# Hymba layer: weight casts and second-stage operands queued behind named matmuls, rotary shuffles issued from ScalarE

## The chip, the cores and the metric

The kernel runs on one core of a Trainium2 chip. The metric is device time in microseconds. A core has TensorE (PE, with its weight loads PEld), VectorE (DVE), ScalarE (ACT), GpSimd (POOL) and SyncE (SP). Every engine takes its instructions from a queue of its own, in order; engines wait for one another by semaphores. A DMA is an instruction in the queue of the engine that issues it, and the data moves on while the engine goes on.

## What is computed

A decoder layer with two groups of heads. The input `x` (1024 x 2048, float32) is projected by `w_in`; one group does sliding-window softmax attention with rotary positions and a sink, the other gated linear attention (GLA) in chunks; both are gated, concatenated, projected by `w_out`, added to the residual and normalized:

```python
h = jnp.einsum('bsd,de->bse', x, w_in[l])
q_a, k_a, v_a, z_a, q_g, k_g, v_g, z_g, gk_lr = jnp.split(h, pts, axis=-1)
qa = _rope(q_a.reshape(B, S, ATT_HEADS, ATT_HEAD_DIM), cos, sin)
ka = _rope(k_a.reshape(B, S, ATT_KV_HEADS, ATT_HEAD_DIM), cos, sin)
y_a = _swa_sink_attention(qa, ka, va, attn_sinks[l]) * jax.nn.silu(z_a)
...
y = jnp.einsum('bse,ed->bsd', jnp.concatenate([y_a, y_g], axis=-1), w_out[l])
x = _layer_norm(DN_ALPHA * x + y, ln_g[l], ln_b[l])
```

## The kernel before

Every float32 product is made of three matmuls on rounded halves: `split` (line 106) casts a tile to its high half (`wh`, `xh`, on ACT, line 112) and subtracts to get the low half (`wl`, `xl`, on DVE, line 113); then hi·hi, hi·lo and lo·hi are summed in PSUM. Weights are loaded by SP into a `raw` buffer of 128 x 1024 (4 buffers, line 102), which holds two tiles; their halves go to a pool of 8 buffers. Activations' halves have 16 buffers.

Stage 1 runs over two halves of the sequence, 512 positions each. `main_f` (line 171) gives a 128 x 512 tile of transposed projections (`acc`, 48 matmuls), `main_v` (line 183) values in the other orientation (`accv`). Between these projections stand the small works on what they gave: `rope` (line 207) copies a projection to `rq` on ACT, shuffles its four groups of 32 rows by four DMAs from SP into `rs` (line 213), and multiplies by cosine on DVE (line 214) and by sine on POOL (line 215). Attention makes scores `ps`, a mask, a maximum `nm`, exponentials on ACT (line 282), a sum `sm`, a scaling of `s` on POOL (line 285), and transposes `pt` on PE (line 288). The GLA part makes decays `w`: an exponential on ACT (line 353), a product on DVE (line 354), and many small `pa` matmuls on PE (line 372). There are 18 calls of `rope`, so 72 shuffle DMAs.

Stage 2 (from line 880) makes the gates `z` (s = 0) and the output projection (s = 1) by Strassen's seven products each, in steps (s, i), with i in the order 1, 6, 7, 4, 2, 5, 3 and 1, 6, 7, 4, 5, 3, 2. Each step has two column halves `fp` and, in each, eight `k`: `w_part` (line 754) loads and splits a weight tile, `product` (line 766) adds three matmuls to `acco` for each row tile, `collect` moves finished sums out of PSUM. The moving operand of a step is a sum of blocks of `x` or of the mixed heads: `y_part` (line 728) loads two or three blocks `yr` by SP, adds them on POOL (line 749, or 746 for i = 3, where a kept sum is loaded), and splits the result. While the second half `fp == 1` of a step is written down, the operands of the next step are made.

The order in each queue is not that of the code: a scheduler simulates the program with its own costs and places each instruction. `tc.high_priority` (as in `split`) lets it place an instruction as early as its inputs and buffers allow. `order(a, b)` tells it that `a` comes after `b`; across engines this adds no wait on the chip, it only changes where `a` stands in its queue.

Of the kernel before, what the change touches and what calls it, by code (L numbers as in the profile page):

```python
# [21 lines left out]
KT = 16  # L22
# [52 lines left out]
def build(ctx: ExitStack, tc, xT, xr, w_e, w_v, w_z, w_gk, w_up, b_gk, cos_d, sin_d, cst_d, sinks, wn_d, w_out, g_d, b_d, out):  # L75
# [30 lines left out]

    def split(src, pool, tag):
        n = src.shape[-1]
        hi = pool.tile([P, 512], F32R, name=tag + "h", tag=tag + "h")[:, :n]
        lo = pool.tile([P, 512], F32R, name=tag + "l", tag=tag + "l")[:, :n]  # L110
        with tc.high_priority():
            A.copy(hi, src)  # L112
            V.tensor_tensor(lo, src, hi.bitcast(F32), ALU.subtract)  # L113
        return hi, lo

# [54 lines left out]
    def main_f(ws, xs):  # L170
        accs = [mm.tile([P, T], F32, name="acc", tag="mm") for _ in ws]
        for k in range(KT):
            xh, xl = xs[k]
            c = slice((k % 4) * P, (k % 4) * P + P)
            for acc, w in zip(accs, ws):
                wh, wl = w[k // 4]
                first = PE.matmul(acc, wh[:, c], xh, start=(k == 0), stop=False)  # L177
                job_head[0] = first if k == 0 else job_head[0]
                PE.matmul(acc, wh[:, c], xl, start=False, stop=False)  # L179
                PE.matmul(acc, wl[:, c], xh, start=False, stop=(k == KT - 1))  # L180
        return accs

    def main_v(w, xs):
        acc = [mm.tile([P, 2, 256], F32, name="accv", tag="mm") for _ in range(2)]
        for k in range(KT):
            wh, wl = w[k // 2]
            c = slice((k % 2) * 256, (k % 2) * 256 + 256)
            xh, xl = xs[k]
            for tb in range(NB):
                o = acc[tb // 2][:, tb % 2]  # L190
                t = slice(tb * P, tb * P + P)
                first = PE.matmul(o, xh[:, t], wh[:, c], start=(k == 0 and tb % 2 == 0), stop=False, skip_group_check=True)  # L192
                job_head[0] = first if k == 0 else job_head[0]
                PE.matmul(o, xh[:, t], wl[:, c], start=False, stop=False, skip_group_check=True)  # L194
                PE.matmul(o, xl[:, t], wh[:, c], start=False, stop=(k == KT - 1), skip_group_check=True)  # L195
        return acc
# [9 lines left out]
    def rope(acc, tabs):  # L206
# [4 lines left out]
        for a in range(4):  # L211
            b = a ^ 1
            SP.dma_start(sw[32 * a:32 * a + 32], q[32 * b:32 * b + 32])
        V.tensor_tensor(q, q, cos, ALU.mult)
# [512 lines left out]

    def y_part(s, i, k):

# [15 lines left out]
        if i == 3:  # L745
            G.tensor_tensor(a, a, raw(kept, "xl"), ALU.add)
        for n, (h, g) in enumerate(more):
            b = raw(block(h, g), "xl" if n % 2 == 0 else "xh")
            G.tensor_tensor(a, a, b, ALU.subtract)  # L749
        if i == 6:  # L750
            A.dma_start(kept, a)
        return split(a, x_p, "x")

# [12 lines left out]
    def product(acc, s, y, w, t, k, first, last):  # L766

        (lh, ll), (rh, rl) = (y, w) if s else (w, y)
        c = slice(t * P, t * P + P)
        PE.matmul(acc, lh[:, c], rh, start=(first and k == 0), stop=False, skip_group_check=True)  # L770
        PE.matmul(acc, lh[:, c], rl, start=False, stop=False, skip_group_check=True)  # L771
        PE.matmul(acc, ll[:, c], rh, start=False, stop=(last and k == 7), skip_group_check=True)  # L772

# [115 lines left out]
    for n, (s, i) in enumerate(seq[:-1]):  # L889
# [11 lines left out]
        for fp in range(2):  # L901
            if i in FIRST:
                accs[fp] = banks(nb)
            for k in range(8):
                if k % 2 == 0:
                    ws = w_part(s, i, fp, k // 2, w_p, "w")
                    for k2 in (k, k + 1):
                        if fp == 1:
                            ys[(*seq[n + 1], k2)] = y_part(*seq[n + 1], k2)
                        elif (s, i, k2) not in ys:  # L910
                            ys[s, i, k2] = y_part(s, i, k2)
# [73 lines left out]
```

## Times and profile before

| | us |
|---|---|
| runs of the kernel before, median of 3 (lowest, highest) | 1478.41 (1468.97, 1479.26) |
| the profiled execution, its own time | 1467.29 |
| its span | 1465.5 |
| TensorE busy | 1398.5 |
| VectorE busy | 888.9 |
| ScalarE busy | 644.1 |
| GpSimd busy | 278.6 |

The span is the stretch that the trace covers; what lies around it is launch and end. Busy time of TensorE contains its slow stretches too: the granted clock over the span is 0.985 of full speed, and where a table of stretches shows less than 1.00, matmuls ran at half the clock for part of it. Stage 1's projections run to 877 us; stage 2 begins there, while the last attention and GLA works are still under way, and its steps end at 1452 us.

### The profile page before, as it was taken

Reading aid. Unit: us, or ns where it says so; the run is one execution under the profiler, and the core shown is the slowest. Engines: PE = TensorE matmul, PEld = TensorE weight load, DVE = VectorE, ACT = ScalarE, POOL = GpSimd, SP = SyncE. Lnnn points to the kernel's source line nnn. Section 1 sums busy time; section 2 is a strip of 40 time slices with the busy share of each in tenths; the row PEclk is TensorE's granted clock in tenths of the full one; section 3 lists DMA queues with packets and bytes.
Section 4 is the critical chain, followed back from the end, with each engine's and each line's share of the span. In section 5 each row is a group of like instructions: output and inputs, shape, how many; then the busy total and the mean of one; then the engine's idle time right before and its main releaser. Section 6 shows DMA issues by size and latency. Waiting matters only on the chain.

```text
span 1465.5 us, 23449 instructions
## 1 busy us (share of the span) xinstructions
PE 1398.5 (95%) x8848; PEld 1163.7 (79%) x8848; DVE 888.9 (61%) x1559; ACT 644.1 (44%) x1405; POOL 278.6 (19%) x269
## 2 busy tenths in 40 slices
PE   8999999999899999999989996999997999999996
PEld 5888879788676888879778775788885888788885
DVE  5555575665666566575665676336475835465798
ACT  5544544544454544544544554246333424433330
POOL 0011131121121111122121224220112032122000
PEclk9999999999999999999999998999999999999998
DMA  8346463645739848464864656777779887766452
GB/s 311 116 141 183 134 182 94 204 137 151 190 111 303 211 158 229 136 185 121 248 156 132 154 145 196 269 202 224 239 263 309 302 256 242 232 216 194 152 214 115
DMA packets 102818, 284.24 MB, mean 194 GB/s; under 512 B 11825, under 2 KB 26161, under 8 KB 101041
## 3 DMA queue, kind: packets, MB, share of 16 engines
q1 hardware_dynamic: 92720, 249.19, 51.1%
q0 software_dynamic: 7680, 29.36, 11.3%
q10 hardware_dynamic: 2304, 4.20, 0.7%
q8 instruction: 69, 1.13, 0.3%
q14 instruction: 45, 0.36, 0.1%
HBM read 250.72 MB, written 85.98 MB: 230 GB/s over the span
## 4 chain that ended last, share of the span: by engine, by line
PE 73%; DMA 12%; DVE 6%; ACT 2%; issue 2%; SPq 2%; POOL 2%; DVEq 0%; POOLq 0%; ACTq 0%
PE acco L770 9%; PE acco L771 9%; PE acco L772 9%; PE acc L177 8%; PE acc L180 8%; PE acc L179 8%; PE accv L195 4%; PE accv L192 4%; PE accv L194 4%; DMA yr<-yd 3%; DMA rs<-rq 2%; PE po L298 2%; DMA yr<-in_xT_dram 2%; DVE wl L113 2%; DMA yr<-ysum 1%
## 5 line engine op out<-in xcount | busy, mean ns | idle before, releaser
L113 DVE TENSOR_TENSOR wl<-raw,wh 128x512 fp32r<-128x512 f32 (+1 forms) x456 | 316.1, 706 | 170.8 <-ACT wh L112 156.4
L112 ACT CAST wh<-raw 128x512 fp32r<-128x512 f32 (+1 forms) x456 | 262.3, 592 | 221.4 <-PE acc L179 111.7
L177 PE MATMUL acc<-xh,wh 128*128 128x512 f32 x704 | 279.4, 398 | 6.9 <-ACT wh L112 6.9
L180 PE MATMUL acc<-xh,wl 128*128 128x512 f32 x704 | 279.2, 397 | 0.0
L179 PE MATMUL acc<-xl,wh 128*128 128x512 f32 x704 | 279.0, 396 | 0.0
L113 DVE TENSOR_TENSOR xl<-yr,xh 128x512 fp32r<-128x512 f32 x112 | 77.3, 691 | 199.2 <-ACT xh L112 198.7
L112 ACT CAST xh<-yr 128x512 fp32r<-128x512 f32 x112 | 69.4, 620 | 276.3 <-POOL yr L749 171.4
L177 PEld LDWEIGHTS acc<-xh,wh 128*128 128x128 f32 x704 | 134.0, 190 | 36.7 <-ACT wh L112 7.9
L770 PE MATMUL acco<-wh,xh 128*128 128x512 f32 x416 | 161.6, 390 | 0.8 <-ACT xh L112 0.8
L771 PE MATMUL acco<-wl,xh 128*128 128x512 f32 x416 | 161.9, 389 | 0.0
L772 PE MATMUL acco<-wh,xl 128*128 128x512 f32 x416 | 161.6, 389 | 0.0
L180 PEld LDWEIGHTS acc<-xh,wl 128*128 128x128 f32 x704 | 133.6, 190 | 30.4 <-issue 2.1
L179 PEld LDWEIGHTS acc<-xl,wh 128*128 128x128 f32 x704 | 134.0, 190 | 28.6 <-issue 1.4
L195 PE MATMUL accv<-wh,xl 128*128 128x256 f32 x512 | 145.2, 284 | 0.0
L192 PE MATMUL accv<-wh,xh 128*128 128x256 f32 x512 | 145.0, 283 | 0.0
L194 PE MATMUL accv<-wl,xh 128*128 128x256 f32 x512 | 144.9, 283 | 0.0
L770 PE MATMUL acco<-xh,wh 128*128 128x512 f32 x336 | 132.6, 397 | 12.1 <-ACT xh L112 6.6
L749 POOL TENSOR_TENSOR yr<-yr 128x512 f32<-128x512 f32 x64 | 86.4, 1350 | 297.0 <-DMA yr<-yd 131.1
L772 PE MATMUL acco<-xh,wl 128*128 128x512 f32 x336 | 132.6, 396 | 0.7 <-DVE wl L113 0.7
L771 PE MATMUL acco<-xl,wh 128*128 128x512 f32 x336 | 132.7, 395 | 0.2 <-DVE xl L113 0.2
L195 PEld LDWEIGHTS accv<-wh,xl 128*128 128x128 f32 x512 | 97.8, 191 | 0.9 <-issue 0.9
L192 PEld LDWEIGHTS accv<-wh,xh 128*128 128x128 f32 x512 | 97.9, 191 | 0.9 <-issue 0.6
(187 smaller groups left out, 2154.6 us busy)
## 6 DMA issues: line engine op xcount, KB each, us to landing
raw<-in_w_e_dram SPq DMA_DIRECT2D x86, 512.0 KB, 4.6
yr<-in_xT_dram SPq DMA_DIRECT2D x88, 256.0 KB, 4.7
yr<-yd SPq DMA_DIRECT2D x88, 256.0 KB, 5.5
raw<-in_w_v_dram SPq DMA_DIRECT2D x32, 512.0 KB, 5.3
raw<-td SPq DMA_DIRECT2D x32, 512.0 KB, 4.8
td<-in_w_z_dram SPq DMA_DIRECT2D x16, 768.0 KB, 6.8
raw<-td SPq DMA_DIRECT2D x32, 384.0 KB, 3.9
raw<-in_w_out_dram SPq DMA_DIRECT2D x24, 512.0 KB, 4.8
```

Source lines behind the costliest of these rows:

```text
L112: A.copy(hi, src)
L113: V.tensor_tensor(lo, src, hi.bitcast(F32), ALU.subtract)
L177: first = PE.matmul(acc, wh[:, c], xh, start=(k == 0), stop=False)
L179: PE.matmul(acc, wh[:, c], xl, start=False, stop=False)
L180: PE.matmul(acc, wl[:, c], xh, start=False, stop=(k == KT - 1))
L192: first = PE.matmul(o, xh[:, t], wh[:, c], start=(k == 0 and tb % 2 == 0), stop=False, skip_group_check=True)
L194: PE.matmul(o, xh[:, t], wl[:, c], start=False, stop=False, skip_group_check=True)
L195: PE.matmul(o, xl[:, t], wh[:, c], start=False, stop=(k == KT - 1), skip_group_check=True)
L749: G.tensor_tensor(a, a, b, ALU.subtract)
L770: PE.matmul(acc, lh[:, c], rh, start=(first and k == 0), stop=False, skip_group_check=True)
L771: PE.matmul(acc, lh[:, c], rl, start=False, stop=False, skip_group_check=True)
L772: PE.matmul(acc, ll[:, c], rh, start=False, stop=(last and k == 7), skip_group_check=True)
```

## The change

Three things are changed. First, `split` with the tag "w" numbers the weight tiles, `used` records the last matmul so far on each, and the ACT cast of tile n is ordered behind the last matmul on tile n-7. Second, the four shuffle DMAs of `rope` are issued from ACT's queue, not from SP's. Third, `product` keeps the latest matmul in `recent`, and a `y_part` made for the next step orders its POOL sums and its ACT cast behind that matmul. The addition for i = 3 moves into the loop of the sums. Instructions are the same in number and kind, but for the 72 issues that move from SP to ACT. All three orders are of the scheduler's kind described above.

```diff
-    def split(src, pool, tag):
+    ends, made = {}, [0]
+
+    def used(n, ins):
+        if n is not None:
+            ends[n] = ins
+
+    def split(src, pool, tag, behind=None):
...
+        if tag == "w":
+            behind = ends.get(made[0] - 7)
+            made[0] += 1
         with tc.high_priority():
-            A.copy(hi, src)
+            ins = A.copy(hi, src)
+            if behind is not None:
+                order(ins, behind)
             V.tensor_tensor(lo, src, hi.bitcast(F32), ALU.subtract)
-        return hi, lo
+        return (hi, lo, made[0] - 1) if tag == "w" else (hi, lo)
...
-                PE.matmul(acc, wl[:, c], xh, start=False, stop=(k == KT - 1))
+                used(n, PE.matmul(acc, wl[:, c], xh, start=False, stop=(k == KT - 1)))
...
-            SP.dma_start(sw[32 * a:32 * a + 32], q[32 * b:32 * b + 32])
+            A.dma_start(sw[32 * a:32 * a + 32], q[32 * b:32 * b + 32])
...
-    def y_part(s, i, k):
+    recent = [None]
+
+    def y_part(s, i, k, behind=None):
...
         if i == 3:
-            G.tensor_tensor(a, a, raw(kept, "xl"), ALU.add)
-        for n, (h, g) in enumerate(more):
-            b = raw(block(h, g), "xl" if n % 2 == 0 else "xh")
-            G.tensor_tensor(a, a, b, ALU.subtract)
+            more = [None]
+        for n, hg in enumerate(more):
+            b = raw(block(*hg) if hg else kept, "xl" if n % 2 == 0 else "xh")
+            ins = G.tensor_tensor(a, a, b, ALU.subtract if hg else ALU.add)
+            if behind is not None:
+                order(ins, behind)
...
-        return split(a, x_p, "x")
+        return split(a, x_p, "x", behind)
...
-        PE.matmul(acc, ll[:, c], rh, start=False, stop=(last and k == 7), skip_group_check=True)
+        recent[0] = PE.matmul(acc, ll[:, c], rh, start=False, stop=(last and k == 7), skip_group_check=True)
+        used(w[2] if len(w) > 2 else None, recent[0])
...
-                            ys[(*seq[n + 1], k2)] = y_part(*seq[n + 1], k2)
+                            ys[(*seq[n + 1], k2)] = y_part(*seq[n + 1], k2, recent[0])
```

The first place is ACT's queue in stage 1, at about 725 us of the profile before: exponentials of the decays (`w_7291` to `w_7634`), weight casts `wh`, and the copy `rq_8106` of a rotation. Before:

```order
L353 ACTIVATE w_7291<-dd_7276 128x512
L248 CAST qs0_7908<-rq_7898 64x512
L248 CAST qs1_7911<-rq_7898 64x512
L112 CAST wh_8222<-raw_8216 128x512
L353 ACTIVATE w_7295<-dd_7276 128x512
L209 COPY rq_8106<-acc_7799 128x512
L353 ACTIVATE w_7299<-dd_7276 128x512
L112 CAST wh_8327<-raw_8325 128x512
L353 ACTIVATE w_7634<-dd_7276 128x512
```

After the change:

```order
L222 COPY rq_8106<-acc_7799 128x512
L226 DMA rs_8108<-rq_8106 32x512
L366 ACT_TABLE_LOAD
L366 ACTIVATE w_7287<-dd_7276 128x512
L226 DMA rs_8108<-rq_8106 32x512
L123 CAST wh_8327<-raw_8325 128x512
L226 DMA rs_8108<-rq_8106 32x512 x2
L366 ACTIVATE w_7291<-dd_7276 128x512
L366 ACTIVATE w_7295<-dd_7276 128x512
L123 CAST wh_8331<-raw_8325 128x512
L366 ACTIVATE w_7299<-dd_7276 128x512
L366 ACTIVATE w_7634<-dd_7276 128x512
```

The casts of weights and of `qs` that stood between the exponentials stand elsewhere, and the four shuffles of `rs_8108` stand behind the copy they read. On PE the `pa` matmuls on `w_7634` stood here before, between the projection's matmuls on `wh_8009` (`acc_8017`):

```order
L372 MATMUL pa_7598<-w_7295 32x32 x16
L372 MATMUL pa_7616<-w_7299 32x32 x16
L177 MATMUL acc_8017<-xh_4884,wh_8009 128x512
L179 MATMUL acc_8017<-xl_4885,wh_8009 128x512
L180 MATMUL acc_8017<-xh_4884,wl_8010 128x512
L177 MATMUL acc_8017<-xh_4889,wh_8009 128x512
L372 MATMUL pa_7716<-w_7634 32x32 x16
```

After the change they stand in the next projection, `acc_8226`:

```order
L190 MATMUL acc_8226<-xh_4853,wh_8212 128x512
L192 MATMUL acc_8226<-xl_4854,wh_8212 128x512
L193 MATMUL acc_8226<-xh_4853,wl_8213 128x512
L385 MATMUL pa_7716<-w_7634 32x32 x16
L381 MATMUL pa_7734<-w_7638 32x32 x8
L190 MATMUL acc_8226<-xh_4858,wh_8212 128x512
```

That is 38 projection matmuls later.

The second place is the transition, on PE: `ps_8973` and `ps_8980` are the scores and `pt_9000` the transposes of one attention tile; `acco` is stage 2's first product. Before, the end of 48 `acco` matmuls that stand between scores and transposes:

```order
L771 MATMUL acco_9507<-xl_9637,wh_9624 128x512
L772 MATMUL acco_9507<-xh_9636,wl_9625 128x512
L770 MATMUL acco_9508<-xh_9636,wh_9624 128x512
L771 MATMUL acco_9508<-xl_9637,wh_9624 128x512
L772 MATMUL acco_9508<-xh_9636,wl_9625 128x512
L288 MATMUL pt_9000<-cst_84,s_8972 128x128 x4
```

After the change:

```order
L279 MATMUL ps_8980<-kh1_96,qs1_8933 128x256
L280 MATMUL ps_8980<-kl1_98,qs1_8933 128x256
L279 MATMUL ps_8980<-kh1_96,qs1_8933 128x256
L280 MATMUL ps_8980<-kl1_98,qs1_8933 128x256
L430 MATMUL pg_9092<-vg0_8559,ah_106 128x256
L431 MATMUL pg_9092<-vg1_8560,ah_106 128x256
L432 MATMUL pg_9092<-vg0_8559,al_108 128x256
L311 MATMUL po_8936<-pm_8970,vt_99 64x128
L301 MATMUL pt_9000<-cst_84,s_8972 128x128 x4
```

There the transposes follow four matmuls behind the scores' last.

The third place is step (0,7) of stage 2. `yr_10017` and `yr_10019` are the two blocks of its second operand, `xh_10022` its cast, `raw_10241` to `raw_10420` weight loads of the step, `wh_10247` a cast of the first of these. SP before:

```order
L763 DMA raw_10090<-td0611_121 128x2x384
L763 DMA raw_10136<-td0611_121 128x2x384
L733 DMA yr_10017<-in_xT_dram 128x512
L733 DMA yr_10019<-in_xT_dram 128x512
L763 DMA raw_10185<-td0700_122 128x2x384
L733 DMA yr_10054<-in_xT_dram 128x512
L763 DMA raw_10213<-td0700_122 128x2x384
L733 DMA yr_10056<-in_xT_dram 128x512
L763 DMA raw_10241<-td0701_123 128x2x384
```

SP after:

```order
L780 DMA raw_10241<-td0701_123 128x2x384
L748 DMA yr_10008<-in_xT_dram 128x512
L748 DMA yr_10010<-in_xT_dram 128x512
L780 DMA raw_10269<-td0701_123 128x2x384
L780 DMA raw_10300<-td0710_124 128x2x384
L748 DMA yr_10017<-in_xT_dram 128x512
L780 DMA raw_10340<-td0710_124 128x2x384
L780 DMA raw_10380<-td0711_125 128x2x384
L748 DMA yr_10019<-in_xT_dram 128x512
L780 DMA raw_10420<-td0711_125 128x2x384
```

The two loads of the operand stood ahead of `raw_10185`, and stand on both sides of `raw_10380` now. ACT after the change, with the evacuations `pre4` and `pre5` of step (0,6):

```order
L123 CAST wh_10243<-raw_10241 128x384
L817 ACTIVATE pre4_9479<-acco_9507 128x512
L817 ACTIVATE pre4_9479<-acco_9508 128x512
L123 CAST wh_10247<-raw_10241 128x384
L817 ACTIVATE pre4_9479<-acco_9509 128x512
L123 CAST xh_10013<-yr_10008 128x512
L123 CAST wh_10271<-raw_10269 128x384
L817 ACTIVATE pre5_9480<-acco_9661 128x512
L817 ACTIVATE pre5_9480<-acco_9662 128x512
L817 ACTIVATE pre5_9480<-acco_9663 128x512
L123 CAST wh_10275<-raw_10269 128x384
L123 CAST xh_10022<-yr_10017 128x512
```

Both casts of operands that step (0,7) begins with stand behind the first evacuations of step (0,6); before, `xh_10013` and `xh_10022` stood 9 and 5 instructions ahead of the first of them.

## Rows read from the trace of the kernel before

**Rows 1.** The page: span, then busy time, share and instructions of each engine.

```profile
span 1465.5 us, 23449 instructions
...
PE 1398.5 (95%) x8848; PEld 1163.7 (79%) x8848; DVE 888.9 (61%) x1559; ACT 644.1 (44%) x1405; POOL 278.6 (19%) x269
```

**Rows 2.** Waits of PE: waited for, us in total, times, longest.

```profile
PE pt L288 <- POOL s L285: 14.5, 4, 8.1
PE pa L372 <- DVE w L354: 13.0, 11, 3.8
PE acco L770 <- ACT xh L112: 7.4, 3, 5.9
...
PE acco L770 <- DVE sza L202: 5.5, 1, 5.5
```

**Rows 3.** Busy us by stretch: width, PE, PEld, DVE, ACT, POOL (instructions), PEclk, DMA share, GB/s.

```profile
922.00:1010.00 88.00, 88.00 (x395) 72.62 (x392) 33.76 (x60) 36.58 (x75) 13.78 (x12) 1.00 0.76 237
...
1105.00:1130.00 25.00, 18.14 (x67) 13.48 (x66) 15.78 (x27) 9.21 (x19) 6.66 (x4) 0.86 0.87 283
1130.00:1452.00 322.00, 321.24 (x1415) 264.89 (x1414) 205.28 (x315) 109.07 (x200) 56.86 (x41) 1.00 0.66 219
```

**Rows 4.** Busy time by stretch, same columns: the places of stage 1, the transition.

```profile
385.00:400.00 15.00, 11.00 (x126) 8.21 (x125) 11.49 (x18) 6.58 (x11) 2.53 (x2) 0.77 0.40 128
464.00:474.00 10.00, 6.84 (x31) 5.68 (x31) 7.39 (x17) 5.13 (x16) 1.30 (x1) 0.86 1.02 362
731.00:741.00 10.00, 6.17 (x111) 4.54 (x110) 7.87 (x13) 2.73 (x5) 2.64 (x3) 0.83 0.49 114
...
904.00:922.00 18.00, 9.90 (x51) 7.82 (x51) 10.50 (x20) 6.25 (x18) 6.04 (x6) 0.70 0.69 210
```

**Rows 5.** Waits of all engines, columns as in rows 2.

```profile
POOL rs L215 <- DMA rs<-rq: 148.0, 17, 14.0
...
ACT wh L112 <- PE acc L179: 111.7, 80, 4.1
...
DVE rq L214 <- DMA rs<-rq: 34.8, 16, 6.7
...
SPq L102 <- DVE wl L113: 391.5, 79, 11.0
```

**Rows 6.** Instructions of line 213 and of tile `ysum`: ns min/median/max, first and last start.

```profile
L213 SPq DMA_DIRECT2D rs<-rq x72: 507/582/1649, 36.6 to 834.5; - x72
...
DMA to landing us min/median/max: 1.9/3.8/14.9
...
L751 ACTq DMA_DIRECT2D ysum<-yr x16: 326/327/353, 877.0 to 1217.0; - x16
```

**Rows 7.** Timeline 905 to 918 us of PE, ACT and POOL: start, us, [idle before].

```profile
917.43 0.90 PE L288 MATMUL pt<-cst,s 128*128 128x128 f32 x3 [8.09 <-POOL s L285]
...
914.36 0.62 ACT L112 CAST xh<-yr 128x512 fp32r<-128x512 f32 x1 [2.42 <-POOL yr L749]
...
916.34 1.04 POOL L285 TENSOR_TENSOR s<-s,sm 128x512 f32<-128x512 f32 x1 [2.01 <-DVE sm L284]
```

**Rows 8.** Groups by line and form: busy, mean ns | idle before; then line 733; a landing.

```profile
L113 DVE TENSOR_TENSOR wl<-raw,wh 128x384 fp32r<-128x384 f32 x112 | 63.1, 587 | 22.7 <-ACT wh L112 22.3
L112 ACT CAST wh<-raw 128x384 fp32r<-128x384 f32 x112 | 53.9, 510 | 23.8 <-PE acco L771 16.5 <-DMA raw<-td 5.0 <-DMA ysum<-yr 1.7
...
L749 POOL TENSOR_TENSOR yr<-yr 128x512 f32<-128x512 f32 x64 | 86.4, 1350 | 297.0 <-DMA yr<-yd 131.1 <-DMA yr<-in_xT_dram 129.8 <-PE acco L772 14.1
...
L112 ACT CAST xh<-yr 128x512 fp32r<-128x512 f32 x112 | 69.4, 620 | 276.3 <-POOL yr L749 171.4 <-POOL yr L746 56.1 <-DMA yr<-yd 22.8
...
L799 ACT ACTIVATE pre<-acco 128x512 f32<-128x512 f32 x12 | 6.8, 597 | 0.0
...
L733 SPq DMA_DIRECT2D yr<-in_xT_dram x88: 327/408/1322, 847.2 to 1126.7; - x88
...
yr<-in_xT_dram SPq DMA_DIRECT2D x88, 256.0 KB, 4.7
```

More of the change, by code (lines that the diff above doesn't have):

```diff
@@ L175, in main_f @@
             for acc, w in zip(accs, ws):
-                wh, wl = w[k // 4]
+                wh, wl, n = w[k // 4]
                 first = PE.matmul(acc, wh[:, c], xh, start=(k == 0), stop=False)
@@ L185, in main_v @@
         for k in range(KT):
-            wh, wl = w[k // 2]
+            wh, wl, n = w[k // 2]
             c = slice((k % 2) * 256, (k % 2) * 256 + 256)
@@ L194, in main_v @@
                 PE.matmul(o, xh[:, t], wl[:, c], start=False, stop=False, skip_group_check=True)
-                PE.matmul(o, xl[:, t], wh[:, c], start=False, stop=(k == KT - 1), skip_group_check=True)
+                used(n, PE.matmul(o, xl[:, t], wh[:, c], start=False, stop=(k == KT - 1), skip_group_check=True))
         return acc
@@ L766, in product @@
     def product(acc, s, y, w, t, k, first, last):
-        (lh, ll), (rh, rl) = (y, w) if s else (w, y)
+        (lh, ll), (rh, rl) = (y, w[:2]) if s else (w[:2], y)
         c = slice(t * P, t * P + P)
```

## Prediction

> **What bounds the kernel now.** I read the page first: its span is 1465.5 us and TensorE is busy for 1398.5 of them [rows 1]. Matmuls set the time, their number is the same after the change, and only two things can be won or lost: idle time of TensorE and time at the half clock. Of the 67 us that are missing, the load of the first operands and the layer norm at the end (about 20 us) are untouched, so some 47 us plus the slow stretches are open. Next come the waits of PE: `pa` matmuls wait 13.0 us for DVE's `w`, `pt` matmuls 14.5 us for POOL's `s`, stage 2's `acco` 7.4 us for ACT's cast of `xh` and 5.5 us for `sza` [rows 2]. Then I cut the span into stretches [rows 3, 4]. The reader should see two things. Steps (0,6) and (0,7), between 922 and 1010 us, lose nothing: 395 matmuls in 88.00 us, 223 ns each. And the losses sit in few places: 385 to 400, 464 to 474 and 731 to 741 in stage 1, the transition 877 to 922, and 1105 to 1130, where step (0,5) gives way to (0,3).
>
> Two waits stand behind those of stage 1. ACT waits 111.7 us for the last matmul on an old weight tile before it may cast the next one into that buffer [rows 5]; whatever is queued behind the cast, the exponentials of `w` among it, waits along, and then DVE, and then `pa`. And the rotation's shuffled copy holds POOL for 148.0 us and DVE for 34.8 [rows 5]; DVE is also the engine that makes `w`.
>
> **The change, part by part.**
>
> *Weight casts behind the last matmul on tile n-7.* The pool has 8 buffers, so a cast must wait for tile n-8 in any case; the edge to n-7 holds nothing up on the chip and only makes the scheduler place the cast later in ACT's queue. In ACT's queue around 725 us four exponentials of `w` stood among five other instructions, and now among one cast; the `pa` matmul on `w_7634` stands 38 projection matmuls later (38 x 223 ns = 8.5 us). At the other two stage-1 losses named above the shift is 9 and 69 matmuls, 2 and 15 us, about as long as the waits there or longer. The three places lose 4.0 + 3.2 + 3.8 = 11.0 us of idle time, the width less PE busy [rows 4], and at granted clocks of 0.77, 0.86 and 0.83 a further 3.5 + 1.4 + 1.7 = 6.6 us at most. With the small `pa` and `pt` waits elsewhere, stage 1 has some 23 us to give. The producers were moved too, though, and any branch that now starts later must still end in its half. I take 15 us; bounds 0 (the waits move to other branch matmuls) and 23.
>
> *Shuffles from ACT's queue.* 72 issues leave SP and join ACT. On SP one took 582 ns in the median; the one kind of transfer that ACT issues today takes 327 [rows 6]. So ACT gains 24 to 42 us of work, in 18 groups of 4, each holding up what is behind it for 1.3 to 2.3 us. ACT is busy for 644 us of 1465.5 [rows 1], and a weight tile is cast several tiles ahead of its use (12 matmuls, 2.7 us, a tile and more), so I cost this at nothing; where that lead is gone it would be 2 us a group. What it gives: the shuffle stands just behind the copy `rq` that it reads, and no longer in a queue where a bulk load waits for DVE's `wl` (391.5 us in all [rows 5]). That gain is inside the 15 us. SP is freed of 72 issues, 42 us.
>
> The Trainium skill, "DMA: Bandwidth & Descriptors", section "Issuing engines are not separate DMA queues", speaks against this part: issuing from several engines saves only the time the sequencer takes to initiate. By that rule the stage-1 term would be about half, 8 us. The rows that bear on it: 0.58 us for an issue, 3.8 from issue to landing, up to 14.9 [rows 6].
>
> *The transition.* POOL's scalings `s` of the last attention tiles now stand ahead of the `y` sums. But in the 8.09 us wait [rows 7] POOL's last wait was for DVE's `sm`, and that was late because ACT, between two exponentials, held 2.42 us for a sum of `y`. Without that hold and the 0.62 of the cast [rows 8] the stop is 5 us. Against it, 48 `acco` matmuls that filled the time between `ps_8973` and `pt_9000` are gone. The same chain from `ps` to `pt`, now with only four small matmuls between its ends, as here, makes a new stop of the same 5 us. Two stops of 5 then stand for one of 8.09, which the half clock followed for longest (904 to 922 at 0.70, so 18 x 0.30 = 5.4 us [rows 4]). The 5.5 us for `sza` stays. I take 0; bounds -13 (the 8.09 gone with its clock, and nothing new) and +6.
>
> *y held back in stage 2.* The sums and casts of step n+1 are placed behind products of step n's second half. Together with the weight edge this makes the scheduler interleave the two halves `fp` of a step: in (0,6), (0,7), (0,5), (0,3), (1,6) and (1,7) `xh` and `wh` now stand directly ahead of their first matmul in the order, where before they had a lead of 34 to 170 matmuls and only (0,3), (1,6) and (1,7) were that tight. Take (0,7), whose second operand pair is needed at stage matmul 3945. Its load `yr_10019` stood seven weight loads further ahead, before `raw_10185`; now it stands behind `raw_10380`. That load waits for a `raw` buffer, so for `wl` of `wh_10247`, and that cast stands on ACT behind two evacuations of step (0,6), the second of which waits for matmul 3916. From there: evacuation 0.60, cast 0.51, `wl` 0.59 [rows 8], two issues of 0.4 each [rows 8], landing 4.7, sum 1.35, cast 0.62 [rows 8] = 9.2 us. There are 29 matmuls x 223 ns = 6.5 us until it is needed: 2.7 us late. The next two pairs hang on the same ring (their loads stand behind `raw_10420`, which waits behind the last evacuation); at 2 us each the step loses 6.7 us and, since stops of this size twice brought the half clock before [rows 4], 1.5 more. By the same walk (0,6) loses 1.5 us (its loads come earlier), (1,6) 1 and (1,7) 4 with its dip. (0,5) to (0,3) was tight before and stays as it was: idle 25 - 18.14 = 6.9 us and clock 0.86, 3.5 us [rows 3]. So stage 2 is 6.7 + 1.5 + 1.5 + 1 + 4 = 14.7 us worse; I count 14, since the walk rounds each step up. Bounds: the steps that were tight before show both ends, 0.8 us idle over 1130 to 1452 and 10.4 at 1105 to 1130 [rows 3]. Four to five steps become tight or tighter: 0 to about 45 us.
>
> *The sum.* -15 + 0 + 14 = -1 us against the profiled execution's 1467.29 us (span 1465.5 and 1.8 around it): 1466. That execution is faster than the lowest of the three runs shown; against their median, 1478.41, it is 1477.
>
> **Rivals.**
>
> *A, faster: stage 1 gives all, and just-in-time operands cost nothing.* For it: (1,6) and (1,7) had the same tight order before and lost 0.8 us [rows 3]; stops of stage 1 vanish when 8 us of cover is put ahead of them. Against it: 1116 us, where a tight `xh` cost 5.9 us in one wait [rows 2]. It gives -23 from stage 1, -4 at the transition and +2 from stage 2, -25: about 1453 on the median's scale.
>
> *B, slower: the ring of `raw` buffers, operand loads and evacuations costs in each tight step what it costs at 1105 to 1130.* The place is SP's queue in (0,6), (0,7), (1,6), (1,7): a `y` load behind a weight load that waits for a cast that waits for the matmuls it should run ahead of. At 8 us a step it is +32, and with -12 from stage 1 +20: 1498. It decides from about 30 us of stops in stage 2, twice my sum. For it: the longest wait for `xh`, 5.9 us [rows 2], and the slow clock at 1105 to 1130 come from one such operand. Against it: 88.00 of 88.00 us in (0,6) and (0,7) show how much slack loads have there today.
>
> *C, the shuffles' move does nothing:* the transfer itself, not its issue or its place in a queue, is the wait. The landing times of up to 14.9 us [rows 6] come from transfers beside bulk loads, and these remain. Then stage 1 gives 8 us, not 15, and the sum is +6: 1484, no change either. (The rule of the Trainium skill's DMA page named above is of this kind; no row here compares two issuing queues for one transfer.)
>
> **How the numbers follow.** My forecast, with gains and losses that cancel, 0.32; C 0.14; A and what lies toward it 0.29; B and what lies toward it 0.25. About 1%, 14.7 us, is what a measurement of this kernel can tell from no change. Forecast and C lie within it, save for 0.02 each way that they may spill; so faster 0.31, same 0.42, slower 0.27. The range reaches to just past A (1449) and B (1503); beyond lie removal of nearly all stops on one side and tight steps at 10 us each on the other. The likeliest case alone spans 1464 to 1490.
>
> **What the profile after would show.** ACT's wait for `acc` (111.7) well down, `rs` on POOL and DVE shorter, no stop over 2 us between 380 and 745; the shuffles as ACT issues of 0.33 to 0.58 us. `pt` at the transition with two stops of 4 to 6 us. In (0,7) PE waits on ACT's `xh`, 2 to 3 us first, in all about 7. Wrong if (0,6) and (0,7) again show a PE busy all the time (then A), if they lose over 20 us (then B), or if the stops at 391, 470 and 737 are still there.

## The result, and the profile after

The changed kernel took 1491.14 us (median of 7 runs, 1487.86 to 1496.67) beside 1478.08 for the kernel before (7 runs, 1467.06 to 1480.12). The ratio is 1.0113, with a 95% interval of 1.0077 to 1.0148. So it is slower, by 13 us between the medians and by 17 by the ratio, where the forecast was no change at 1477; 1491 lies inside the range given, just above the 1490 where the likeliest case ended. The profiled execution of the change has a span of 1487.3 us, that of before 1465.5 [rows 1]. Their difference, 21.8 us, is larger than that of the medians, since the profiled execution of before took 1467.29 us, close to the lowest of its runs. Single places may be read from the two traces, while gains and losses of a few us in total must be read from the ratios.

The page of the change, span and busy time:

```profile
span 1487.3 us, 23313 instructions
...
PE 1408.7 (95%) x8848; PEld 1169.1 (79%) x8848; DVE 891.2 (60%) x1559; ACT 645.0 (43%) x1405; POOL 275.5 (19%) x269
```

TensorE is busy 10 us longer with the same matmuls and idle 12 us longer. Most of the 10 is time at the half clock: 0.981 of full speed was granted over the span, 0.985 before, so by estimate 28 us were lost to the slow clock in place of 22 (0.019 and 0.015 of the two spans). Its waits (waited for, us in total, times, longest) answer to [rows 2]:

```profile
PE acco L787 <- ACT xh L123: 21.0, 11, 4.8
PE pa L385 <- DVE w L367: 11.6, 9, 2.1
PE pt L301 <- POOL s L298: 9.6, 3, 5.5
...
PE acco L787 <- DVE sza L215: 4.7, 1, 4.7
PE acco L788 <- DVE xl L126: 4.2, 5, 3.0
PE pk L417 <- DVE kq L413: 3.1, 1, 3.1
PE lracc L335 <- DMA raw<-in_xT_dram: 1.9, 1, 1.9
...
ACT wh L123 <- PE acc L192: 95.8, 61, 4.2
```

The reader should see one line that grew threefold, the cast of the second stage's operand: 7.4 us in 3 waits before, 21.0 in 11 now. The wait for `xl`, the low half of the same operands, is 4.2 us and was 0.2. `pa` fell from 13.0 to 11.6 only, and two waits are new, `pk` and `lracc`. The last line is ACT's wait for old weight tiles, 111.7 us before [rows 5]. Cut by stage (width, busy time of PE, PEld, DVE, ACT, POOL with instructions, granted clock, DMA share, GB/s; the first row is stage 1 to its last projection matmul, the second the transition, the third the rest of stage 2), and with (0,6) and (0,7) apart, which answer to [rows 3]:

```profile
6.00:871.00 865.00, 844.06 (x6395) 710.37 (x6396) 525.46 (x980) 425.48 (x964) 159.28 (x172) 0.99 0.60 173
871.00:925.00 54.00, 40.07 (x199) 31.86 (x198) 30.17 (x68) 20.92 (x69) 14.06 (x13) 0.87 0.32 97
925.00:1475.00 550.00, 524.46 (x2258) 426.83 (x2256) 326.62 (x501) 196.16 (x370) 100.40 (x74) 0.98 0.70 229
...
936.00:1018.00 82.00, 70.20 (x288) 54.68 (x287) 29.51 (x47) 28.33 (x59) 22.55 (x17) 0.96 0.68 218
```

The same three cuts of before:

```profile
7.00:877.00 870.00, 844.42 (x6412) 710.30 (x6413) 538.29 (x994) 429.98 (x975) 164.88 (x176) 0.99 0.59 172
877.00:928.00 51.00, 36.95 (x181) 29.20 (x181) 29.73 (x57) 20.66 (x60) 19.74 (x16) 0.83 0.63 187
928.00:1453.00 525.00, 516.72 (x2259) 424.06 (x2257) 311.62 (x497) 190.58 (x366) 92.29 (x67) 0.99 0.71 232
```

Idle PE is the width less PE's busy time: 25.6, 14.0 and 8.3 us before, 20.9, 13.9 and 25.5 after. Stage 1 won 5 us of width, the transition lost 3, stage 2 lost 25. Part of the 5 is only moved: 17 matmuls fewer stand in the first cut and 18 more in the second. Steps (0,6) and (0,7), which had no idle time before [rows 3], are 11.8 us idle here, and their 288 matmuls take 82.3 us in place of 65.3.

The 4.83 us stop in step (0,6) and the 2.09 us stop in step (0,7), on SP, POOL, ACT and PE (start, us, instruction, idle time before and its releaser):

```profile
953.74 0.38 SPq L780 DMA_DIRECT2D raw<-td  x1
954.24 3.21 SPq L748 DMA_DIRECT2D yr<-in_xT_dram  x6
...
961.55 5.51 POOL L764 TENSOR_TENSOR yr<-yr 128x512 f32<-128x512 f32 x4 [6.70 <-DMA yr<-in_xT_dram]
...
964.19 0.62 ACT L123 CAST xh<-yr 128x512 fp32r<-128x512 f32 x1 [8.27 <-POOL yr L764]
...
964.86 1.65 PE L787 MATMUL acco<-xh,wh 128*128 128x512 f32 x3 [4.83 <-ACT xh L123]
...
971.33 4.01 SPq L780 DMA_DIRECT2D raw<-td  x2
975.39 0.46 SPq L748 DMA_DIRECT2D yr<-in_xT_dram  x1
...
979.99 1.26 POOL L764 TENSOR_TENSOR yr<-yr 128x512 f32<-128x512 f32 x1 [3.90 <-DMA yr<-in_xT_dram]
...
981.29 0.62 ACT L123 CAST xh<-yr 128x512 fp32r<-128x512 f32 x1 [1.91 <-POOL yr L764]
...
981.96 0.96 PE L787 MATMUL acco<-xh,wh 128*128 128x512 f32 x3 [2.09 <-ACT xh L123]
```

From the second half down this is the chain that the prediction walked: a weight load that stands for its buffer until 975.3, behind it the operand's load, 4.6 us to landing, the sum, the cast, and PE.

### The profile page after: what moved, and what is told of

It is laid out like the page before. It is cut to its first block, busy times and chain, and to the rows that moved or that the text cites. A ratio compares the mean times of both kernels' runs of the same rounds, so it can differ in the third digit from the quotient of the medians.

```text
span 1487.3 us, 23313 instructions
## 1 busy us (share of the span) xinstructions
PE 1408.7 (95%) x8848; PEld 1169.1 (79%) x8848; DVE 891.2 (60%) x1559; ACT 645.0 (43%) x1405; POOL 275.5 (19%) x269
## 4 chain that ended last, share of the span: by engine, by line
PE 73%; DMA 10%; DVE 7%; ACT 4%; issue 3%; POOL 1%; SPq 1%; ACTq 1%; DVEq 0%; POOLq 0%
PE acco L787 9%; PE acco L788 9%; PE acco L789 9%; PE acc L192 8%; PE acc L190 8%; PE acc L193 8%; PE accv L208 4%; PE accv L205 4%; PE accv L207 4%; DMA yr<-in_xT_dram 4%; DMA rs<-rq 2%; PE po L311 2%; POOL yr L764 1%; DVE wl L126 1%; DVE dd L368 1%
## 5 line engine op out<-in xcount | busy, mean ns | idle before, releaser
L126 DVE TENSOR_TENSOR wl<-raw,wh 128x512 fp32r<-128x512 f32 (+1 forms) x456 | 320.7, 715 | 167.8 <-ACT wh L123 162.0
L123 ACT CAST wh<-raw 128x512 fp32r<-128x512 f32 (+1 forms) x456 | 263.9, 592 | 244.9 <-PE acc L192 95.8
L764 POOL TENSOR_TENSOR yr<-yr 128x512 f32<-128x512 f32 x80 | 108.9, 1365 | 374.4 <-DMA yr<-in_xT_dram 144.7
L126 DVE TENSOR_TENSOR xl<-yr,xh 128x512 fp32r<-128x512 f32 x112 | 82.8, 740 | 158.1 <-ACT xh L123 157.7
L787 PE MATMUL acco<-wh,xh 128*128 128x512 f32 x416 | 157.3, 392 | 2.2 <-ACT xh L123 2.2
L789 PE MATMUL acco<-wh,xl 128*128 128x512 f32 x416 | 155.3, 390 | 0.1
L787 PE MATMUL acco<-xh,wh 128*128 128x512 f32 x336 | 128.0, 405 | 23.7 <-ACT xh L123 18.8
L789 PE MATMUL acco<-xh,wl 128*128 128x512 f32 x336 | 127.9, 399 | 0.0
```

The source lines that it names most:

```text
L123: ins = A.copy(hi, src)
L764: ins = G.tensor_tensor(a, a, b, ALU.subtract if hg else ALU.add)
L789: recent[0] = PE.matmul(acc, ll[:, c], rh, start=False, stop=(last and k == 7), skip_group_check=True)
```

## The experiments

The theory to begin with: the operand edge alone makes the losses of stage 2, and weight edge and shuffles give a few us in stage 1. The rivals: the weight edge makes casts late in stage 2; or the shuffles' issues hold up ACT. Each table row below is the median of the runs and the ratio to the kernel before on the same chip; the last columns are PE's idle time, width less busy time, by the three cuts of one profiled execution.

| kernel | median us | ratio, 95% interval | stage 1 | transition | stage 2 |
|---|---|---|---|---|---|
| before | 1478.08 | 1 | 25.6 | 14.0 | 8.3 |
| whole change | 1491.14 | 1.0113, 1.0077 to 1.0148 | 20.9 | 13.9 | 25.5 |
| operand edge alone | 1490.13 | 1.0105, 1.0074 to 1.0136 | 26.7 | 12.8 | 23.6 |
| weight edge alone | 1470.72 | 0.9970, 0.9950 to 0.9990 | 29.3 | 12.3 | 9.6 |
| shuffles alone | 1461.71 | 0.9909, 0.9875 to 0.9943 | 17.8 | 14.2 | 8.5 |
| shuffles alone, again | 1463.34 | 0.9937, 0.9904 to 0.9970 | 22.7 | 14.1 | 9.2 |
| weight edge, shuffles | 1470.83 | 0.9984, 0.9959 to 1.0009 | 23.9 | 15.1 | 9.7 |
| shuffles, weight edge on 200 tiles | 1474.39 | 1.0001, 0.9986 to 1.0016 | 28.2 | 17.7 | 9.1 |
| shuffles, weight edge n-8 | 1468.38 | 0.9950, 0.9934 to 0.9967 | 22.9 | 14.6 | 10.4 |
| shuffles, weight edge n-6 | 1471.55 | 0.9976, 0.9952 to 1.0000 | 23.9 | 14.7 | 8.5 |
| shuffles, operand edge 8 k back | 1462.79 | 0.9906, 0.9871 to 0.9940 | 20.2 | 15.1 | 11.7 |
| whole, operand edge 8 k back | 1469.27 | 0.9956, 0.9932 to 0.9979 | 21.9 | 14.6 | 9.9 |
| shuffles, operand edge, operand loads first | 1479.04 | 1.0029, 1.0009 to 1.0049 | 18.2 | 10.7 | 31.4 |
| shuffles, operand loads first | 1460.26 | 0.9898, 0.9871 to 0.9924 | 15.2 | 15.0 | 11.6 |
| shuffles on POOL | 1475.74 | 1.0003, 0.9982 to 1.0023 | 27.2 | 16.1 | 10.7 |
| shuffles, 72 other issues on SP | 1477.71 | 1.0018, 0.9996 to 1.0040 | 30.8 | 14.0 | 9.7 |
| shuffles, 72 issues and waits on SP | 1475.04 | 1.0000, 0.9979 to 1.0020 | 26.7 | 15.1 | 13.0 |

The two profiles of the shuffles alone differ by 4.9 us in stage 1, so one profile's stage 1 is good for some 5 us and no more. The stop of `pt` near 466 us was 0.81 us in the one and 3.81 in the other.

### One part at a time

The operand edge alone:

```diff
-            behind = ends.get(made[0] - 7)
...
-            A.dma_start(sw[32 * a:32 * a + 32], q[32 * b:32 * b + 32])
+            SP.dma_start(sw[32 * a:32 * a + 32], q[32 * b:32 * b + 32])
```

> Only the third part of the change: sums and casts of the next step's operands behind the latest product; weight casts and shuffles as before. Theory (the operand edge alone makes the losses of stage 2): stage 2 from the end of the transition on is 20 to 30 us longer than before, in the same steps (0,6), (0,7), (1,7) as with the whole change, stage 1 as before within 3 us; 1492 to 1508. Rival (the weight edge delays the weight casts and they are late in the tight steps): about as before, 1470 to 1482, no stops for xh in (0,6) and (0,7).

Measured 1490.13 us, 1.0105: as much as the whole change, and a little below the range expected. Its waits of PE and its stage 2 (columns as above):

```profile
PE acco L786 <- ACT xh L122: 20.2, 11, 4.2
...
931.00:1477.00 546.00, 522.39 (x2255) 426.25 (x2254) 322.80 (x500) 198.50 (x370) 103.20 (x74) 0.98 0.71 229
```

Stage 2 is 21 us longer than before with 23.6 us idle, and the wait for `xh` is that of the whole change. The theory holds in the main; with the weight casts as they were before, they cannot be the reason. (0,6) lost 6.2 us and (0,7) 6.8. (1,7), which I had named too, lost nothing, and (0,3), which I had not, lost 8.5.

The weight edge alone, against the change:

```diff
-                            ys[(*seq[n + 1], k2)] = y_part(*seq[n + 1], k2, recent[0])
+                            ys[(*seq[n + 1], k2)] = y_part(*seq[n + 1], k2)
...
-            A.dma_start(sw[32 * a:32 * a + 32], q[32 * b:32 * b + 32])
+            SP.dma_start(sw[32 * a:32 * a + 32], q[32 * b:32 * b + 32])
```

> Only the first part: weight casts behind the last matmul on tile n-7; operands and shuffles as before. Theory: stage 2 as before within 3 us, stage 1 and the transition 3 to 10 us shorter; 1466 to 1476. Rival (the weight edge costs stage 2): 10 us or more lost in (0,6) to (1,7), 1485 or more.

Measured 1470.72 us, 0.9970. The interval allows a gain of 1 to 7 us. Its profile, of an execution that took 1479.80 us, shows none of it in stage 1, where idle time was 29.3 us, so where the gain sits stays open. Stage 2 is left alone, as the theory had it.

The shuffles alone:

```diff
-            behind = ends.get(made[0] - 7)
...
-                            ys[(*seq[n + 1], k2)] = y_part(*seq[n + 1], k2, recent[0])
+                            ys[(*seq[n + 1], k2)] = y_part(*seq[n + 1], k2)
```

> Only the second part: the 72 shuffle DMAs issued from ACT. Theory: waits of POOL and DVE for rs fall, the time moves by less than 5 us either way (1471 to 1483). Rival 1 (the move is what gave the 6 us of stage 1): stage 1 ends 5 to 8 us earlier. Rival 2 (the issues hold up ACT's casts): 5 us or more slower, with PE waiting for wh or w in stage 1.

Measured 1461.71 us, 0.9909, and once more, as the control of two later runs:

> The shuffles from ACT alone once more, as the control for the next two on the same chip: 1456 to 1466.

1463.34 us, 0.9937. My theory gave the shuffles nothing either way; they are the part that gains, 9 to 13 us (the two intervals together allow 4 to 18). The waits of PE, and stage 1, of the first of the two profiles:

```profile
PE pt L300 <- POOL s L297: 9.4, 2, 8.6
PE pa L384 <- DVE w L366: 8.7, 10, 1.9
...
7.00:868.00 861.00, 843.25 (x6410) 709.33 (x6410) 534.78 (x992) 429.03 (x974) 166.04 (x176) 0.99 0.60 174
```

`pa` waits 8.7 us and not 13.0, and its long wait of 3.8 us is gone [rows 2]. `pt` waits 9.4 us and not 14.5, but 13.0 in the second profile, and its longest wait, 8.6 us, is no shorter than the 8.1 of before. The issues cost ACT what they cost SP, as the instructions of the shuffles' line in the whole change show; they answer to [rows 6]:

```profile
L226 ACTq DMA_DIRECT2D rs<-rq x72: 514/592/1646, 37.5 to 831.8; - x72
...
DMA to landing us min/median/max: 1.9/4.0/8.3
```

Landing takes 4.0 us in the median and took 3.8. So the transfer got no faster. The longest landing fell from 14.9 to 8.3 us, but it is 7.5 us with the weight edge alone too, where SP issues the shuffles.

Weight edge and shuffles together, the change without its third part:

```diff
-                            ys[(*seq[n + 1], k2)] = y_part(*seq[n + 1], k2, recent[0])
+                            ys[(*seq[n + 1], k2)] = y_part(*seq[n + 1], k2)
```

> The change without its third part. Theory: stage 1 ends 4 to 8 us earlier than before, stage 2 as before within 3 us, 1468 to 1475, so 13 to 25 us faster than the whole change. Rival (operands held back are needed for what stage 1 and the transition gained, or weight edge and shuffles cost in stage 2): 1480 or more.

Measured 1470.83 us, 0.9984. That is 20 us faster than the whole change, and by the ratios 7 to 11 slower than the shuffles alone. The two parts do not add; the edge takes most of the shuffles' gain back. (The interval lies clear of that of the first run of the shuffles, and overlaps a little with that of the second.)

### Is it that operands are late?

The operand edge to an earlier product, with the shuffles on ACT:

```diff
+    past = []
...
+        past.append(recent[0])
...
-                            ys[(*seq[n + 1], k2)] = y_part(*seq[n + 1], k2, recent[0])
+                            ys[(*seq[n + 1], k2)] = y_part(*seq[n + 1], k2, past[max(-1 - 8 * nb, -len(past))])
```

> Shuffles on ACT and the operand edge, but to a product eight k earlier (half a step, so that an operand can be made a whole half step sooner). In the order the leads of xh in (0,6) and (0,7) come back to 83 and 27 matmuls in the mean (29 and 0 with the edge to the latest product, 116 and 68 without). Theory (lateness of operands is what stage 2 pays for): the losses of (0,6) and (0,7) fall from 13 to 0 to 5 us, total 1462 to 1472. Rival (any such edge costs because it ties POOL and ACT to PE's progress): 10 us or more remain in these two steps, total 1475 or more.

Measured 1462.79 us, 0.9906, the level of the shuffles alone. In its profile, of an execution that took 1471.43 us, (0,6) lost nothing, (0,7) still 7 us, which is more than expected, and (0,3) gained 4. The same edit on the whole change:

> The whole change, but with the operand edge to a product eight k earlier. Leads of xh in the order: (0,6) 82 instead of 28, (0,7) 16 instead of 0. Theory (the operands' lateness is what the third part costs, and it adds to the rest): 8 to 16 us faster than the whole change, 1474 to 1482; (0,6) loses nothing, (0,7) 3 to 8 us. Rival (with the weight edge the steps stay tight anyway): 1486 or more.

Measured 1469.27 us, 0.9956, so 22 us faster than the whole change. Its wait for `xh` and its stretch over (0,6) and (0,7) (934 us and on):

```profile
PE acco L788 <- ACT xh L123: 7.3, 3, 3.5
...
934.00:1003.00 69.00, 69.00 (x306) 57.15 (x305) 28.01 (x49) 29.61 (x61) 15.47 (x12) 1.00 0.81 257
```

No idle time, and 7.3 us of waits for `xh` in place of 21.0. An edge of the same kind, eight `k` earlier, costs nothing that these medians show: it is lateness, not the edge. I had expected 1474 us or more here and (0,7) to lose 3 to 8 us, and it lost none. The lead in the order is no full measure of lateness: (0,7) lost nothing with a mean lead of 16 matmuls here, and 7 us with 27 in the run before.

Operand edge and shuffles, with a step's weight loads behind its operand loads on SP:

```diff
+    loads = {}
...
-                SP.dma_start(r, src)
+                loads[s, i, k // 2] = SP.dma_start(r, src)
...
-            SP.dma_start(r, src[:, (q % 2) * m:(q % 2) * m + m].rearrange("p (u c) -> p u c", u=2))
+            ins = SP.dma_start(r, src[:, (q % 2) * m:(q % 2) * m + m].rearrange("p (u c) -> p u c", u=2))
+            at = (s, i, q if fp == 0 else 3)
+            if at in loads:
+                order(ins, loads[at])
```

> Shuffles on ACT and the operand edge as in the change, and one more edge: a step's weight loads stand on SP behind the loads of the operands that they are used with. Leads in the order: xh in (0,7) 18 matmuls instead of 0, in (0,4) 65 instead of 4, but wh 20 instead of 53. Theory (an operand's load stands behind a weight load that waits): the waits for xh in (0,7) fall by half or more and the steps from (0,6) to (0,7) lose 3 to 8 us instead of 13. Rival (the sums and casts themselves, tied to the last product, are late, whatever the loads do): 11 us or more in these two steps.

Measured 1479.04 us, 1.0029. Its waits of PE:

```profile
PE acco L790 <- ACT wh L122: 29.7, 5, 9.9
PE pt L300 <- POOL s L297: 9.2, 3, 5.4
```

The waits for `xh` are gone from the top, and waits for weights, up to 9.9 us, stand there. (0,7) lost nothing; (0,6) lost 13.8 us and (0,5) 14.5. By its number the rival won; by what PE waited for, the load's place on SP is what made `xh` late in (0,7), and this place makes the weights late instead: SP's operand loads now stand 47.0 us for the old `xl` in their buffers (15.6 before), with the weight loads behind them. The same order without the operand edge:

> Shuffles on ACT, no operand edge, no weight edge, but weight loads of a step on SP behind the operand loads that they are used with. The lead of xh in (0,3), which was 3 matmuls before, is 23 in the order. Theory (the losses where (0,5) gives way to (0,3) come from an operand whose load stands late): these 10 us fall to 0 to 4, total 1451 to 1458. Rival (that operand is late for its kept sum, or the weights, with a lead of 0 in (1,6), are late instead): 1460 to 1470.

Measured 1460.26 us, 0.9898, the lowest of all kernels here, though not to be told from the shuffles alone. (0,5) and (0,3) did not gain: by its profile they take 4 us more than before. A lead of 23 matmuls in place of 3 did not help, so that expectation was wrong, and why (0,3) stops stays open.

### What the weight edge takes back

```diff
-            behind = ends.get(made[0] - 7)
+            behind = ends.get(made[0] - 7) if made[0] < 200 else None
```

> Shuffles on ACT and the weight edge for the first 200 tiles alone, so for none of the last tiles before the transition and none of stage 2. In the order 40 acco matmuls are back between ps_8973 and pt_9000 (0 with the edge on all tiles, 48 before). Theory (the weight edge loses at the transition what it wins): the stretch from projection end to matmul 3744 is 4 us or more shorter than with shuffles and all weight edges; 1456 to 1466. Rival (the weight edge itself undoes the shuffles' gain in stage 1, where branches only wait elsewhere): stage 1 and the total stay those of shuffles with all weight edges, 1467 to 1474.

Measured 1474.39 us, 1.0001. The filler between scores and transposes was back, and the transition was no shorter: idle 17.7 us. The loss is not the transition's, and the theory fell.

The edge to another tile (`made[0] - 8`, then `made[0] - 6`), shuffles on ACT:

> Shuffles on ACT and the weight edge, but to tile n-8, whose buffer the cast takes anyway. In the order the mean lead of a weight cast in stage 1 is 89 matmuls as without the edge (85 with n-7), and pt_9000 stands at matmul 3696 as without it. Theory (what the weight edge costs is that casts, and with them the small matmuls of attention and GLA, are placed later): as shuffles alone, 1456 to 1465. Rival (any edge from the casts to PE makes a worse order, whichever tile it names): 1468 to 1476, as with n-7.

> As the run with n-8, but the edge names tile n-6: mean lead in stage 1 74 matmuls, the small matmuls later still. Theory: slower than with n-7, 1472 to 1485, more idle time of PE in stage 1 than the 20 us with n-7. Rival (later casts free ACT for the exponentials, as the prediction had it): 1455 to 1468.

Measured 1468.38 us (0.9950) and 1471.55 (0.9976), beside 0.9984 with n-7 and 0.9909 and 0.9937 without. With n-8 the casts' lead is that of no edge, and by the ratios 2 to 6 us of the gain are gone, but the interval overlaps with both of the shuffles alone, so a loss isn't shown. With n-6 the lead is much shorter, and no more is lost than with n-7. So it is not, or not mainly, how late the casts stand. The loss goes better with how far PE's order changes. Of the 6640 matmuls ahead of step (0,6), at least 23 stand in another order than with the shuffles alone where the edge names n-8, 614 with n-7, 786 with n-6, and 603 with the edge on 200 tiles (counted from the traces, by the names of tiles without their numbers). Which of these moves costs the time is not shown. One stop of stage 1 with weight edge and shuffles shows how a gain turns into another wait (ACT's issues of one rotation, then DVE and PE):

```profile
636.08 1.16 ACTq L226 DMA_DIRECT2D rs<-rq  x2
...
637.51 1.07 ACTq L226 DMA_DIRECT2D rs<-rq  x1
...
638.64 0.64 ACTq L226 DMA_DIRECT2D rs<-rq  x1
...
645.90 0.69 DVE L227 TENSOR_TENSOR rq<-rq,cos 128x512 f32<-128x512 f32 x1 [5.09 <-DMA rs<-rq]
...
648.94 0.63 PE L417 MATMUL pk<-cst,kq 128*128 128x128 f32 x4 [2.94 <-DVE kq L413]
```

The four issues stand apart, with casts and an exponential between; the last is out 3.2 us after the first began, DVE stands for its landing until 645.90 with `kq` queued behind, and PE waits 2.94 us for `pk`. This stop is in the whole change too (3.1 us in the waits above) and in neither profile of the shuffles alone.

### What the shuffles' move saves

From POOL's queue instead:

```diff
-            A.dma_start(sw[32 * a:32 * a + 32], q[32 * b:32 * b + 32])
+            G.dma_start(sw[32 * a:32 * a + 32], q[32 * b:32 * b + 32])
```

> The 72 shuffles issued from POOL's queue, nothing else changed. Theory (the shuffles' move gains because SP is rid of 72 issues, so its stores and loads go out earlier): faster than before by 5 to 13 us although each issue costs POOL about 1 us: 1461 to 1470. Rival (it gains because the issue stands right behind the copy on ACT): no gain or slower, 1472 to 1485.

Measured 1475.74 us, 1.0003: no gain, as the rival had it. This doesn't settle it, for POOL pays for what SP is rid of: its multiplications by sine now stand in one queue with the issues, and POOL stands 61.8 us for the copy.

So SP got its load back while the shuffles stay on ACT, first issues alone, then issues that wait for the copy. The 72 transfers go to a spare buffer that nothing reads:

```diff
-        A.copy(q, acc)
+        first = A.copy(q, acc)
...
             A.dma_start(sw[32 * a:32 * a + 32], q[32 * b:32 * b + 32])
+            ins = SP.dma_start(spare[32 * a:32 * a + 32, turns[0] * 512:turns[0] * 512 + 512], cst[32 * b:32 * b + 32, :512])
+            order(ins, first)
```

In the second run they read `q` in place of `cst`, without the `order`.

> Shuffles on ACT, and SP gets 72 other transfers of the same size in their place, from a constant tile to a spare buffer in DRAM, so with issues but no wait for ACT's copy. Theory (SP's issue time, 42 us, is what the move saves): the gain is gone, 1470 to 1480. Rival (the place on ACT right behind the copy, or the wait on SP, is what counts): 1456 to 1466, as the control.

Measured 1477.71 us, 1.0018, where the control on the same chip took 1463.34.

> As the run before, but SP's 72 transfers read the rotation's copy, so SP waits for ACT's copy again, 58 us in all, as it did before the change, while the real shuffles go out from ACT. Theory (SP standing still for the copy, with loads and stores behind it, is what the move saves): 1470 to 1480 where the run with issues alone stays near the control. Rival (only the shuffles' own place counts): 1456 to 1466.

Measured 1475.04 us, 1.0000. Both lose the gain, and the wait for the copy adds nothing to the issues. The second is no clean test of that wait: DVE and POOL stand 12.6 and 42.6 us for the added transfers, which read the copy that the rotation works on. The line of the 72 issues, the waits of PE and stage 1 of the first of the two:

```profile
L228 SPq DMA_DIRECT2D spare<-cst x72: 302/423/1708, 32.5 to 829.9; - x72
...
PE pg L434 <- DVE on L469: 11.7, 3, 6.6
PE pa L389 <- DVE w L371: 9.5, 7, 2.3
...
7.00:881.00 874.00, 843.19 (x6400) 709.25 (x6400) 533.37 (x993) 430.31 (x978) 164.60 (x176) 0.99 0.61 178
```

With 72 issues of 423 ns on SP, 30 us, the kernel takes 14 us more by the medians, 12 by the ratios. But the waits that return are not those that went: `pa` stays at 9.5 us and `pg`, 2.8 us with the shuffles alone, waits 11.7. The 72 transfers also move 4.7 MB more, and the scheduler makes another order for PE: of the 6640 matmuls ahead of step (0,6) at least 536 stand elsewhere than with the shuffles alone, and 552 in the second run. Moving the shuffles had changed the place of 283. So the runs agree with the theory that the gain needs SP free of the 72 issues, but don't show it. The rival, that the gain is that of another order on PE, is left by all of them: the five lowest rows of the table, 0.9898 to 0.9950, are those whose order up to (0,6) is that of the shuffles alone but for 23 matmuls or fewer. (One more row has that order, the operand edge with operand loads first, and loses its time behind it, in stage 2.) To part the two, the order would have to be held while the issues move.

## Why the prediction was wrong, point by point

**Stage 1, -15 us: the step that failed.** I read ACT's wait of 111.7 us for old weight tiles [rows 5] as the reason of the `pa` waits, and credited the weight edge for moving small matmuls behind 8 us of cover. Weight edge and shuffles without the third part measured 0.9984, a gain of 2 us (between a loss of 1 and a gain of 6) where I had 15. The matmuls did move, and ACT's wait fell to 95.8 us, but stage 1 has 20.9 us of idle PE where it had 25.6, a difference within the scatter of one profile. Of the three stops that I named, the 3.16 us at 470 are gone and the 3.83 at 737 are 1.84, but 2.03 at 391 are 2.10 at 395, and stops at `pk` and `lracc` came. The waits for `rs` fell as I had said, POOL's from 148.0 to 116.1 us and DVE's from 34.8 to 27.2, and little of it reached PE. I take it that the producers moved too; that was the lower bound's reason, and it should have been the value. By the runs the edge alone gives 4 us, and beside the shuffles it takes 7 to 11 us of their 9 to 13. What did give is the part that I costed at nothing of its own. I took the shuffles' gain to be that they stand behind their copy; the runs point to SP's issues instead, the 42 us that I had worked out and then left without a price, but the changed order on PE explains them as well, so this cause stays open.

**Rival C and the rule of the Trainium skill.** "DMA: Bandwidth & Descriptors", section "Issuing engines are not separate DMA queues", says that only the sequencer's issue time is saved. The traces agree that the transfer is no faster, 4.0 us to landing against 3.8. What I and rival C drew from it, a smaller gain of this part, was wrong: moving the issues came with 9 to 13 us, with landing as before. Whether it was the issue time that gave them is not shown.

**The transition, 0 us.** Right in the main. `pt` stops twice, where I had two stops of 5:

```profile
888.72 1.11 PE L301 MATMUL pt<-cst,s 128*128 128x128 f32 x4 [5.50 <-POOL s L298]
...
914.41 0.66 PE L301 MATMUL pt<-cst,s 128*128 128x128 f32 x4 [3.54 <-POOL s L298]
```

`sza` stops for 4.69 us where I had 5.5. Idle time is 13.9 us against 14.0. The width is 3 us more, for 18 matmuls more stand in it.

**Stage 2, +14 us: right mechanism, sized too small.** It measured +25 in width, and by the ratios the operand edge costs 15 us alone and 19 on top of the other two parts. In (0,7) the walk was close: I had the second pair 2.7 us late and it was 2.09, I had 8.2 us for the step and it was 8.0. (1,7) measured 2.9 us where I had 4, but that is luck: with the operand edge alone it lost nothing, and with the shuffles alone, which have no such edge, 2.3 us in one profile. (1,6), where I had 1, lost nothing. The term that was mis-sized is (0,6): 1.5 us, "its loads come earlier". They did not. Its operands are sums of three blocks, six loads stand behind one weight load at 953.74, and the sum that the cast waits for ends 2.6 us after the landing; it cost 1.4 + 7.7 = 9.1 us. The rest is the entry to (0,5), 3.1 us, which I had at nothing, and 1.6 at (0,3).

**The sum.** -15 + 0 + 14 became -5 + 3 + 25 in the profiles, 22 by the spans, and +13 in the medians. By the ratios of the parts it is -2 for weight edge and shuffles and +19 for the operand edge: stage 1 is the larger miss, 13 us, and stage 2 adds 5 of the same sign. Rival B had the place right, a `y` load behind a waiting weight load on SP, and its 8 us a step fit (0,6) and (0,7). They do not fit (1,6) and (1,7), and its own signs, over 20 us in (0,6) and (0,7) and about 30 us of stops in stage 2, were not reached: 17 and 25.5. I gave it 0.25, and the whole of it would have been 1498. Its own objection, that (0,6) and (0,7) have slack today, was no objection, for the slack belonged to the order that the change replaced.

## What to carry to other kernels

An order given to a scheduler as an edge to "the latest" work leaves little lead or none (0 matmuls in the mean in (0,7) here): half a step earlier it cost nothing that the medians show (here 22 us between the two). Price a move of issues from one queue to another even where the queue isn't busy in the profile's sense; the 72 shuffles were the largest gain of this change, and they were hidden in the sum. Where several orders are changed at once, cost each alone: of three parts here one gained 9 to 13 us, one gave 4 alone and took most of that back beside it, and one lost 15. And where a scheduler places the instructions, look at what else an edit moved before its effect is put down to the edit: 72 transfers added to SP moved at least 536 matmuls on PE.

## What was not expected of the hardware

Nothing that the runs show. Open is the queue: 72 issues of 0.42 us on SP, which stands 391.5 us for `wl` alone [rows 5], came with 14 us more, though the issuing engine is never the one that PE is said to wait for. These runs do not tell whether the time is that of the issues or that of the other order on PE.
